# Where the accumulating transfers for w_out's sums are issued

## The chip, the cores and the metric

The kernel runs on one NeuronCore of a Trainium2 chip. The metric is the device time of one execution in microseconds (us). The core has five engines that work side by side, each through its own instructions in order: PE (matrix products), DVE and ACT (elementwise work on SBUF, the on-chip memory), POOL (elementwise work, and here also the issue of accumulating DMA transfers) and SP (issue of plain DMA transfers). Sixteen DMA engines carry all transfers. They are fed from two queues that matter here: q1, which SP fills, and q0, which POOL fills. Engines wait for each other through semaphores.

## The reference

One encoder layer on 256 tokens of width 2048, everything in fp32:

```python
hn = rmsnorm(x, norm_w)
q, v, f_fwd, f_bwd, z_a, b_gate, c_gate, h_b, z_b = split(hn @ w_in)   # nine times 2048 columns
o_a = head_rmsnorm(hgrn2_bidirectional(silu(q), v, f_fwd, f_bwd)) * silu(z_a)   # group A
y_b = b_gate * conv3(c_gate * h_b)                                              # group B
o_b = rmsnorm(y_b) * silu(z_b)
h = x + concat(o_a, o_b) @ w_out
h = h + (p @ w_ple) * sigmoid(h @ w_ple_gate)
out = rmsnorm(h, final_norm_w)
```

The weights are 151 MB for w_in, 34 MB for w_out and 17 MB for w_ple_gate; each element is read once and used for 256 tokens.

## The kernel before

**Products.** An fp32 product is made of split operands: a weight tile is cut in a rounded high part and the rest (`split`, line 121 on ACT, line 122 on DVE), the activations likewise, and PE multiplies high by both and rest by high. `Stream` brings the weights: raw tiles of 1 MB in a ring of three (`rawp`, SP's DMAs at lines 96 and 100), split tiles in a ring of five (`splp`). A raw tile can be loaded again only when the last part of the tile three before it has been split, and a split tile only when PE has used what was there. `Stream.get` splits three parts ahead of PE.

**Stages.** First group A (up to about 510 us in the trace), then group B (to about 855 us), then w_out, then the gate. Group B runs over i = 0 to 7, 256 columns each. A *column-major block* is one call of `gemm_in`: 2 MB of weights of one kind (C, h, B or Z) for one i, PE lines 431 and 433, whose loads move 8 KB per partition and packet. Blocks i = 0 and 1 make all four kinds this way. For i = 2, 4 and 6 a *wide block* (`gemm_ch`, `gemm_pair`, `half`, PE lines 560 to 562) makes C and h for i and i + 1 at once: eight raw tiles (quarters), of which the third and the fifth go through a scheme of seven products in place of eight, for which DVE adds weight blocks (line 83) ahead of the last two of their four splits. A wide block's loads move 2 KB packets, those of the two quarters with sums 1 KB packets; a wide block is followed by the column-major blocks B and Z of i and of i + 1. The wide block takes all four of the PSUM banks that the column-major blocks use in turn.

**Sums for w_out.** Four of the eight quarters of each half of w_out also go through seven products. Their weight sums are not made by DVE but by DMA in DRAM, ahead of time: sixteen pairs (`prepared`, tiles `sums{u}_{half}_{q}`). During group A, SP copies the right and left blocks into `sums` (`prepare`, line 337). During group B, POOL issues three accumulating transfers per pair (`add_up`): step 0 adds w_out to two blocks (line 345, 512 KB), steps 1 and 2 add a block of `sums` to another (line 349, 256 KB each). Each step waits on POOL until the pair's step before has landed. In the w_out stage SP loads `sums` as raw tiles.

**Order.** POOL executes in the order in which its instructions stand in the program. `pump()` takes the next of the 48 steps from `steps_up` and places it there; `at(dt, fn)` runs fn after dt ticks, and a tick is one step in PE's list of products (four products in a column-major block, three in most of a wide one). A transfer's place decides behind which POOL instruction it stands; nothing else makes it wait, apart from the landing of the step before. In the kernel before `pump()` stands behind POOL's products of group B (lines 965 to 1002), and four times at ticks 5, 15, 25 and 35 of each wide block (line 948), where POOL has no other work.

Of the kernel before, what the change touches and what calls it, by code (L numbers as in the profile page):

```python
# [137 lines left out]
def tile_hymba_encoder(  # L138
# [75 lines left out]
    oblocks, prepared = [], []  # L214
# [109 lines left out]
    pend = []  # L324
    now, count = [0], [0]

    def at(dt, fn):
        count[0] += 1
        pend.append((now[0] + dt, count[0], fn))
# [9 lines left out]
    def add_up(what, step):  # L339
        (_, right), sums = what  # L340
        if step == 0:
            n = right[0].shape[2]
            for c, src in enumerate(right):
                tc.keep_in_program_order(
                    pool.dma_start(sums[:, 0:3:2, n * c : n * c + n], src, accum_op=ALU.add)
                )
        else:
            dst, src = ((3, 0), (1, 3))[step - 1]
            tc.keep_in_program_order(pool.dma_start(sums[:, dst], sums[:, src], accum_op=ALU.add))


    steps_up = [(4 * g + n, step) for g in range(len(prepared) // 4) for step in range(3) for n in range(4)]

    def pump():
        if steps_up:
            n, step = steps_up.pop(0)
            add_up(prepared[n], step)
# [104 lines left out]
    def gemm_pair(name, sums_of, ids, get):  # L462

        acc = [psg.tile([P, 512], F32, tag="g", name=f"a{name}_{b}") for b in range(4)]
        sc = [t.rearrange("p a b -> p (a b)") for t in scps]

        def extra():
            x, y = (psm.tile([P, 512], F32, tag=t, name=f"e{t}{name}") for t in "xy")
            return [x, y, *sc]

        main = [[acc[m], acc[2 + m]] for m in range(2)]
        for q1, q5, q6, q7 in half(main, extra, VZ_ORDER, sums_of, ids, xs, xq, True):
            vt, zt, d = get()
            with tc.high_priority(offset=400):
                act.copy(out=vt[:, 0], in_=q1)
                dve.tensor_tensor(out=d, in0=vt[:, 0], in1=q6, op=ALU.subtract)
                dve.tensor_tensor(out=zt[:, 0], in0=q5, in1=d, op=ALU.subtract)
                dve.tensor_tensor(out=vt[:, 1], in0=d, in1=q7, op=ALU.subtract)
                dve.tensor_tensor(out=zt[:, 1], in0=zt[:, 0], in1=q7, op=ALU.add)
        with tc.high_priority(offset=400):  # L480
            for n, dst in enumerate((vt, zt)):
                for m in range(2):
                    dve.tensor_tensor(out=dst[:, m], in0=main[m][n], in1=dst[:, m], op=ALU.add)
        return vt, zt
# [9 lines left out]
    def evac(acc, dst, tmpp, offset=200):  # L494

        with tc.high_priority(offset=offset):
            for m in range(2):
                r = tmpp.tile([P, T], F32, tag="r", name="r", bufs=2)
                act.copy(out=r, in_=acc[m][:, 1, :])  # L499
                dve.tensor_tensor(out=dst(m), in0=acc[m][:, 0, :], in1=r, op=ALU.add)  # L500
# [10 lines left out]
    with tc.manual_schedule(engines={ENG.Activation, ENG.DVE, ENG.PE}):  # L511
        for g in range(4):
            for c in range(3):
                half, v = ws.open(ids3[c][g])

                n = 2 if g or c else 1
# [309 lines left out]
    last_two, kept = [None], []  # L826
# [104 lines left out]
    def convolved(i, ut):  # L931

        for ii in (i, i + 1):
            tp = psm.tile([P, 2, T], F32, tag="xy"[ii % 2], name=f"ut{ii}")
            for h in range(2):
                c = (2 * (ii % 2) + h) * P
                for m in range(2):
                    pe.transpose(tp[:, h, m * P : (m + 1) * P], ut[:, m, c : c + P], ident)
            act.copy(out=ub[ii % 2][:, :, 1 : T + 1], in_=tp)

    def gemm_ch(i):

        def get():
            a, b = (bp.tile([P, 2, 512], F32, tag=f"late{e}", name=f"ch{i}_{e}") for e in range(2))
            return a, b, early[:, 0:512]

        for z in range(4):
            at(5 + 10 * z, pump)
        a, b = gemm_pair(f"ch{i}", CH_SUMS, blocks[B_CG, i], get)
        with tc.high_priority(offset=300):  # L950
            for m in range(2):
                dve.scalar_tensor_tensor(
                    out=a[:, m], in0=a[:, m], scalar=rx2[:, m : m + 1], in1=b[:, m], op0=ALU.mult, op1=ALU.mult
                )
        at(12, lambda: convolved(i, a))

    for i in range(8):
        u = ub[i % 2]
        if i < 2:
            cg = ctmp.tile([P, 2, T], F32, tag="cg", name=f"cg{i}", bufs=2)  # L960
            evac(gemm_in(B_CG, i, {} if i else TURNED), lambda m: cg[:, m, :], ctmp)
            hb = ctmp.tile([P, 2, T], F32, tag="hb", name=f"hb{i}", bufs=2)
            evac(gemm_in(B_HB, i, {} if i else TURNED), lambda m: hb[:, m, :], ctmp)
            by_norms(cg, rbc2, 2)
            pump()
            pool.tensor_tensor(out=u[:, :, 1 : T + 1], in0=cg, in1=hb, op=ALU.mult)
            pump()
        elif i % 2 == 0:
            gemm_ch(i)
        kick = {} if i % 2 else TURNED  # L970
        hb = ctmp.tile([P, 2, T], F32, tag="hb", name=f"bg{i}", bufs=2)
        evac(gemm_in(B_BG, i, kick), lambda m: hb[:, m, :], ctmp)
        if i >= 2:
            cg = ctmp.tile([P, 2, T], F32, tag="cg", name=f"cg{i}", bufs=2)
        for m in range(2):
            ct = 2 * i + m
            dve.tensor_scalar(cg[:, m, :], u[:, m, 0:T], cvw[:, 0, ct : ct + 1], None, op0=ALU.mult)
            for j in (1, 2):
                dve.scalar_tensor_tensor(
                    out=cg[:, m, :], in0=u[:, m, j : j + T], scalar=cvw[:, j, ct : ct + 1],  # L980
                    in1=cg[:, m, :], op0=ALU.mult, op1=ALU.add,
                )
        pool.tensor_tensor(out=cg, in0=cg, in1=hb, op=ALU.mult)  # L983
        pump()
        y2 = ctmp.tile([P, 2, T], F32, tag="tmp", name=f"y2_{i}")
        act.activation(y2, cg, AF.Square)
        pool.tensor_tensor(out=ysum, in0=ysum, in1=y2, op=ALU.add)
        pump()
        hb = ctmp.tile([P, 2, T], F32, tag="hb", name=f"zb{i}", bufs=2)
        evac(gemm_in(B_ZB, i, kick), lambda m: hb[:, m, :], ctmp, 500 if i in (1, 3, 5) else 200)  # L990
        by_norms(hb, rbc, 2)
        pump()
        sz = ctmp.tile([P, 2, T], F32, tag="tmp", name=f"szb{i}")
        act.activation(sz, hb, AF.Sigmoid)
        for m in range(2):
            ct = 2 * i + m
            dve.scalar_tensor_tensor(
                out=hb[:, m, :], in0=hb[:, m, :], scalar=cnw[:, ct : ct + 1], in1=sz[:, m, :],
                op0=ALU.mult, op1=ALU.mult,
            )  # L1000
        pool.tensor_tensor(out=cg, in0=cg, in1=hb, op=ALU.mult)
        pump()
        if i == 0:
            assert not pend
            actx.close()
            bp = mctx.enter_context(tc.tile_pool(name="bp", bufs=1, side="right", reuse_waits="tile"))
            og = bp.tile([P, 2, 2, 2, P], F32, name="og")
            suma = bp.tile([P, len(SUMS), 3, 2, P], F32R, name="suma")
            mixb.extend(bp.tile([P, 2, 2, T], F32R, name=f"mixb{i}") for i in range(6))
        if i == 6:  # L1010
            mixb.extend(bp.tile([P, 2, 2, T], F32R, tag=f"late{e}", name=f"mixb{i + e}") for e in range(2))
        if i == 2:
            for e in range(2):
                act.copy(out=og[:, e], in_=kept[e])
        hi, lo = mixb[i][:, :, 0, :], mixb[i][:, :, 1, :]
        act.copy(out=hi, in_=cg)
        dve.tensor_tensor(out=lo, in0=cg, in1=hi, op=ALU.subtract)
        for src, z, n in ((mixa, i - 1, len(SUMS)), (mixb, i - SUMS[0], len(sumb32))):
            if 0 <= z < n:
                k = 2 * SUMS[z]  # L1020
                a = ctmp.tile([P, 2, T], F32, tag="tmp", name=f"sa{i}")
                if src is mixb:
                    act_sums(mixb[k // 2], a, sumb32[z])
                else:
                    t = ctmp.tile([P, 4, P], F32, tag="hb", name=f"sb{i}", bufs=2)
                    act_sums(mixa[:, k : k + 2], a, t)
                    act_split(suma[:, z], mixa[:, k : k + 2], t)
# [282 lines left out]
```

## Time and profile before

| | |
|---|---|
| median of 3 runs | 1125.66 us (1125.65 to 1126.28) |
| profiled execution | 1123.09 us, its span 1121.4 us |
| PE busy | 1102.3 us, 98% of the span |
| DVE, ACT, POOL busy | 889.1, 684.9, 246.9 us |
| q1 (SP) | 242.25 MB, 62.1% of the 16 engines' span |
| q0 (POOL) | 16.78 MB, 10.1% |

Views used: the groups of waits, the chain of waits (followed back from the last instruction), the timeline of one engine (start, duration, what it did, and in brackets its idle time ahead and what ended it), the table by stage (length, busy time of each engine, granted TensorE clock, share of DMA engines busy, GB/s) and the DMA view of a stretch (packets, MB and share per queue; then issues by kind with the median time from issue to landing). PE's pieces in the timeline overlap, so its pace is read from the distance of starts.

### The profile page before, as it was taken

The numbers are of one execution on the slowest core, as the hardware profiler recorded it, in microseconds if no ns is written. First come the engines' busy times: TensorE is split into PE (matmuls) and PEld (weight loads), VectorE is DVE, ScalarE is ACT, GpSimd is POOL, SyncE is SP. The second block draws the span as 40 slices with busy tenths as digits, with TensorE's granted clock in tenths as the row PEclk, the third lists the DMA queues.
The fourth block names the chain that finished last, engine by engine and source line by source line (L and its number), as shares of the span: only waits on it lengthen the run. The fifth ranks groups of instructions, "written<-read, shape, count | busy, mean of one in ns | idle before, by whom it ended". The sixth has DMA issues, their size and how long they took to land.

```text
span 1121.4 us, 16647 instructions
## 1 busy us (share of the span) xinstructions
PE 1102.3 (98%) x6269; PEld 939.9 (84%) x6269; DVE 889.1 (79%) x1164; ACT 684.9 (61%) x943; POOL 246.9 (22%) x203
## 2 busy tenths in 40 slices
PE   9999999999999999999998998999999999999996
PEld 8888888888888888888887886887888888888886
DVE  7798588997889788996686797787878879877673
ACT  7696578567866787656444454454556565565562
POOL 1144024203620343053240250132041000000011
PEclk9999999999999999999999998999999999999999
DMA  9886675586548654668887789599779987887532
GB/s 349 322 269 214 219 249 184 176 294 208 187 157 293 227 192 161 215 206 232 232 183 269 212 207 261 193 235 227 257 208 286 339 284 283 301 291 260 201 132 76
DMA packets 83248, 260.43 MB, mean 232 GB/s; under 512 B 8160, under 2 KB 23904, under 8 KB 68704
## 3 DMA queue, kind: packets, MB, share of 16 engines
q1 hardware_dynamic: 73920, 242.25, 62.1%
q0 software_dynamic: 8960, 16.78, 10.1%
q8 instruction: 49, 0.80, 0.3%
q10 hardware_dynamic: 288, 0.34, 0.1%
q14 instruction: 31, 0.25, 0.1%
HBM read 257.25 MB, written 35.65 MB: 261 GB/s over the span
## 4 chain that ended last, share of the span: by engine, by line
PE 90%; DMA 4%; DVE 3%; ACT 2%; SPq 1%; POOL 0%; issue 0%; DVEq 0%; ACTq 0%; POOLq 0%
PE a L433 29%; PE a L431 15%; DMA raw<-in_w_in_dram 3%; PE avz L560 3%; PE avz L562 3%; PE avz L561 3%; PE pg L1071 3%; PE pg L1072 3%; PE pg L1070 3%; PE ach L561 2%; PE ach L562 2%; PE ach L560 2%; DVE spl L122 1%; PE pa L561 1%; PE pa L562 1%; PE pa L560 1%
## 5 line engine op out<-in xcount | busy, mean ns | idle before, releaser
L122 DVE TENSOR_TENSOR spl<-raw,spl 128x1024 fp32r<-128x1024 f32 (+2 forms) x431 | 518.1, 1217 | 148.9 <-ACT spl L121 145.1
L121 ACT CAST spl<-raw 128x1024 fp32r<-128x1024 f32 (+2 forms) x431 | 423.4, 994 | 282.6 <-PE a L431 69.1
L433 PE MATMUL a<-xs,spl 128*128 128x512 f32 x1408 | 483.8, 395 | 0.0
L431 PE MATMUL a<-xs,spl 128*128 128x256 f32 x1408 | 376.6, 278 | 0.0
L433 PEld LDWEIGHTS a<-xs,spl 128*128 128x128 f32 x1408 | 259.9, 188 | 55.3
L431 PEld LDWEIGHTS a<-xs,spl 128*128 128x128 f32 x1408 | 262.5, 188 | 5.6
L560 PE MATMUL ach<-spl,xs 128*128 128x512 f32 x156 | 62.7, 402 | 7.0 <-ACT spl L121 7.0
L1187 POOL TENSOR_TENSOR hh<-hh,fw 128x512 f32<-128x512 f32 (+1 forms) x9 | 11.0, 1228 | 251.0 <-ACT gt L1186 248.4
L561 PE MATMUL ach<-spl,xs 128*128 128x512 f32 x156 | 62.8, 403 | 2.3 <-DVE spl L122 2.3
L562 PE MATMUL ach<-spl,xs 128*128 128x512 f32 x156 | 62.6, 401 | 0.0
L560 PE MATMUL avz<-spl,xs 128*128 128x512 f32 x138 | 54.0, 391 | 0.0
L562 PE MATMUL avz<-spl,xs 128*128 128x512 f32 x138 | 53.7, 389 | 0.0
L561 PE MATMUL avz<-spl,xs 128*128 128x512 f32 x138 | 53.7, 389 | 0.0
L983 POOL TENSOR_TENSOR cg<-cg,bg 128x512 f32<-128x512 f32 x8 | 11.2, 1406 | 189.6 <-DVE bg L500 189.6
L499 ACT COPY r<-a 128x256 f32<-128x256 f32 x88 | 31.5, 368 | 31.8 <-PE a L431 31.7
L1070 PE MATMUL pg<-spl,ht 128*128 128x512 f32 (+1 forms) x120 | 45.2, 377 | 0.0
L1071 PE MATMUL pg<-spl,ht 128*128 128x512 f32 (+1 forms) x120 | 45.0, 375 | 0.0
L1072 PE MATMUL pg<-spl,ht 128*128 128x512 f32 (+1 forms) x120 | 45.0, 375 | 0.0
L733 POOL TENSOR_TENSOR qc<-pf,ge 128x256 f32<-128x256 f32 x16 | 21.0, 1313 | 106.7 <-ACT dd L723 91.8
L560 PEld LDWEIGHTS ach<-spl,xs 128*128 128x128 f32 x156 | 30.4, 195 | 14.7 <-ACT spl L121 8.3
L83 DVE TENSOR_TENSOR raw<-raw 128x512 f32<-128x512 f32 (+1 forms) x45 | 41.2, 915 | 0.8
L122 DVE TENSOR_TENSOR spl<-early,spl 128x1024 fp32r<-128x1024 f32 (+1 forms) x29 | 32.9, 1147 | 9.3 <-ACT spl L121 8.7
(378 smaller groups left out, 1892.5 us busy)
## 6 DMA issues: line engine op xcount, KB each, us to landing
raw<-in_w_in_dram SPq DMA_DIRECT2D x82, 1024.0 KB, 5.0
raw<-in_w_in_dram SPq DMA_DIRECT2D x196, 256.0 KB, 4.4
raw<-in_w_out_dram SPq DMA_DIRECT2D x36, 512.0 KB, 5.7
sums<-in_w_out_dram SPq DMA_DIRECT2D x32, 512.0 KB, 7.1
raw<-in_w_in_dram SPq DMA_DIRECT2D x26, 512.0 KB, 5.8
raw<-sums SPq DMA_DIRECT2D x13, 1024.0 KB, 6.4
raw<-in_w_gate_dram SPq DMA_DIRECT2D x9, 1024.0 KB, 5.6
sums<-in_w_out_dram POOLq DMA_DIRECT2D x16, 512.0 KB, 13.0
```

The lines of the kernel that those rows point to most:

```text
L83: self.nc.vector.tensor_tensor(out=out, in0=out, in1=other, op=ALU.add)
L121: self.nc.scalar.copy(out=v[:, :, 0], in_=r)
L122: self.nc.vector.tensor_tensor(out=v[:, :, 1], in0=r, in1=v[:, :, 0], op=ALU.subtract)
L431: pe.matmul(a[:, :T], lhsT=lhsT, rhs=xs[:, kt, 0, :], start=False, stop=(kt == NKT - 1))
L433: pe.matmul(a, lhsT=lhsT, rhs=xs[:, kt, :, :].rearrange("p s n -> p (s n)"), start=(kt == 0), stop=False)
L499: act.copy(out=r, in_=acc[m][:, 1, :])
L560: pe.matmul(acc, lhsT=ah, rhs=w[:, 0], start=start, stop=False)
L561: pe.matmul(acc, lhsT=ah, rhs=w[:, 1], start=False, stop=False)
L562: pe.matmul(acc, lhsT=al, rhs=w[:, 0], start=False, stop=stop)
L1070: pe.matmul(acc[m], lhsT=lh, rhs=wh, start=(kt == 0), stop=False)
L1071: pe.matmul(acc[m], lhsT=lh, rhs=wl, start=False, stop=False)
L1072: pe.matmul(acc[m], lhsT=ll, rhs=wh, start=False, stop=(kt == nk - 1))
```

## The change

The 48 steps keep their number, kind and size. `steps_up` takes eight pairs in turn, not four, so eight step 0 come ahead of the first step 1. The pumps behind POOL's products and in the wide blocks go away. Instead `pumps(t0, t1, n)` spreads n steps over ticks t0 to t1: 10 and 12 in the four column-major blocks of i = 0 and 1, and 9, 9 and 8 in those that follow the wide blocks of i = 2, 4 and 6.

```diff
-    steps_up = [(4 * g + n, step) for g in range(len(prepared) // 4) for step in range(3) for n in range(4)]
+    steps_up = [(8 * g + n, step) for g in range(len(prepared) // 8) for step in range(3) for n in range(8)]
...
     def gemm_ch(i):
...
-        for z in range(4):
-            at(5 + 10 * z, pump)
         a, b = gemm_pair(f"ch{i}", CH_SUMS, blocks[B_CG, i], get)
...
+    def pumps(t0, t1, n):
+        for z in range(n):
+            at(t0 + (t1 - t0) * z // (n - 1), pump)
+
     for i in range(8):
         u = ub[i % 2]
         if i < 2:
+            pumps(2, 55, 10 + 2 * i)
...
             by_norms(cg, rbc2, 2)
-            pump()
             pool.tensor_tensor(out=u[:, :, 1 : T + 1], in0=cg, in1=hb, op=ALU.mult)
-            pump()
         elif i % 2 == 0:
             gemm_ch(i)
+        if i >= 2 and i % 2 == 0:
+            pumps(2, 41, 9 if i < 6 else 8)
...
         pool.tensor_tensor(out=cg, in0=cg, in1=hb, op=ALU.mult)
-        pump()
...
         pool.tensor_tensor(out=ysum, in0=ysum, in1=y2, op=ALU.add)
-        pump()
...
         by_norms(hb, rbc, 2)
-        pump()
...
         pool.tensor_tensor(out=cg, in0=cg, in1=hb, op=ALU.mult)
-        pump()
```

The assertion that nothing is pending at the end of i = 0 gives way to another. The order of instructions on PE, DVE, ACT and SP stays as it is; POOL's alone changes, at three kinds of places.

**Block i = 0.** POOL's work for the last head pair of group A (`kx7`, then `s7`, the masked scores that PE's products `o` read) and for group B's i = 0 (`ub0`). Before:

```order
L739 TENSOR_TENSOR kx7_4678<-kc7_4672,ge7_4659 128x512
L801 TENSOR_TENSOR s7_4891<-early_152 128x256
L966 TENSOR_TENSOR ub0_4621<-cg0_4627,hb0_4763 128x2x256
L345 DMA sums0_0_3_82<-in_w_out_dram 256x1x512
L801 TENSOR_TENSOR s7_4891<-early_152 128x256
L983 TENSOR_TENSOR cg0_4627<-cg0_4627,bg0_4908 128x512
L345 DMA sums0_0_4_83<-in_w_out_dram 256x1x512
```

and with the change:

```order
L739 TENSOR_TENSOR kx7_4679<-kc7_4673,ge7_4660 128x512
L345 DMA sums0_0_3_82<-in_w_out_dram 256x1x512
L345 DMA sums0_0_4_83<-in_w_out_dram 256x1x512
L345 DMA sums0_0_5_84<-in_w_out_dram 256x1x512
L345 DMA sums0_1_2_85<-in_w_out_dram 256x1x512
L345 DMA sums0_1_3_86<-in_w_out_dram 256x1x512
L801 TENSOR_TENSOR s7_4897<-early_152 128x256
L968 TENSOR_TENSOR ub0_4621<-cg0_4627,hb0_4766 128x2x256
L345 DMA sums0_1_4_87<-in_w_out_dram 256x1x512
L801 TENSOR_TENSOR s7_4897<-early_152 128x256
L345 DMA sums0_1_5_88<-in_w_out_dram 256x1x512
L986 TENSOR_TENSOR cg0_4627<-cg0_4627,bg0_4912 128x512
```

With the change five step 0 stand between `kx7` and `s7`, and two more follow ahead of the product with i = 0's B gate (the eighth, pair 1's, stands further up, ahead of group A's last output gate); before, one step 0 stood between the two `s7` and one ahead of `kx7`.

**From i = 0 to i = 1**, POOL with the change (before, one transfer stands between each two of these products):

```order
L1001 TENSOR_TENSOR cg0_4627<-cg0_4627,zb0_5029 128x512
L349 DMA sums0_0_4_83<-sums0_0_4_83 128x512
L349 DMA sums0_0_5_84<-sums0_0_5_84 128x512
L349 DMA sums0_1_2_85<-sums0_1_2_85 128x512
L349 DMA sums0_1_3_86<-sums0_1_3_86 128x512
L349 DMA sums0_1_4_87<-sums0_1_4_87 128x512
L349 DMA sums0_1_5_88<-sums0_1_5_88 128x512
L349 DMA sums0_0_2_81<-sums0_0_2_81 128x512
L504 TENSOR_TENSOR cg1_5150<-cg1_5150,early_152 128x512
L968 TENSOR_TENSOR ub1_4622<-cg1_5150,hb1_5243 128x2x256
L349 DMA sums0_0_3_82<-sums0_0_3_82 128x512
```

Six step 1 and the first step 2 stand ahead of the product by the norms (`cg1`), which `ub1`, the input of the convolution of i = 1, needs.

**From i = 1 to the wide block of i = 2.** Before:

```order
L1001 TENSOR_TENSOR cg1_5146<-cg1_5146,zb1_5429 128x512
L349 DMA sums0_0_5_84<-sums0_0_5_84 128x512
L345 DMA sums0_1_2_85<-in_w_out_dram 256x1x512
L345 DMA sums0_1_3_86<-in_w_out_dram 256x1x512
L345 DMA sums0_1_4_87<-in_w_out_dram 256x1x512
L345 DMA sums0_1_5_88<-in_w_out_dram 256x1x512
L983 TENSOR_TENSOR cg2_5955<-cg2_5955,bg2_5854 128x512
```

and with the change:

```order
L1001 TENSOR_TENSOR cg1_5150<-cg1_5150,zb1_5439 128x512
L349 DMA sums0_1_4_87<-sums0_1_4_87 128x512
L349 DMA sums0_1_5_88<-sums0_1_5_88 128x512
L345 DMA sums1_0_2_89<-in_w_out_dram 256x1x512
L345 DMA sums1_0_3_90<-in_w_out_dram 256x1x512
L986 TENSOR_TENSOR cg2_5965<-cg2_5965,bg2_5860 128x512
```

Between POOL's last product of i = 1 and its first one behind the wide block there stand two small and two large transfers, where one small and four large ones stood. At the wide block of i = 4 it is one large and three small ones, at that of i = 6 three small ones; before, one small and four large ones stood at each.

More of the change, by code (lines that the diff above doesn't have):

```diff
@@ L1001, in tile_hymba_encoder @@
         pool.tensor_tensor(out=cg, in0=cg, in1=hb, op=ALU.mult)
-        pump()
         if i == 0:
-            assert not pend
+            assert kept
             actx.close()
```

## The prediction

> **What bounds the kernel now.** I read the page first, then the groups of waits for PE, then the table by stage over the three wide blocks.
>
> ```profile
> span 1121.4 us, 16647 instructions
> PE 1102.3 (98%) x6269; PEld 939.9 (84%) x6269; DVE 889.1 (79%) x1164; ACT 684.9 (61%) x943; POOL 246.9 (22%) x203
> PE ach L560 <- ACT spl L121: 7.0, 3, 2.7
> PE ach L561 <- DVE spl L122: 2.3, 3, 0.8
> 566.96:614.52 47.56, 44.33 (x188) 36.00 (x187) 36.46 (x44) 22.17 (x27) 8.80 (x8) 0.96 0.88 237
> 659.84:708.93 49.09, 45.65 (x189) 36.91 (x187) 37.89 (x50) 22.61 (x28) 8.80 (x8) 0.93 0.91 240
> 754.26:799.65 45.39, 42.75 (x189) 34.84 (x188) 34.19 (x37) 21.92 (x25) 8.64 (x8) 1.00 0.94 256
> 577.17 0.39 PE L560 MATMUL ach<-spl,xs 128*128 128x512 f32 x1
> 581.25 0.39 PE L560 MATMUL ach<-spl,xs 128*128 128x512 f32 x1
> ```
>
> PE sets the time nearly everywhere. Inside the program it waits 9.3 us, all in the wide blocks, once in each. The three stages do the same work and differ in length, and the third column from the right, the granted clock, says that two of the waits also cost speed afterwards (0.96 and 0.93 against 1.00). A wide block is 62 groups of three products (six quarters of eight, two of seven), 186 starts. The last two rows are 18 starts apart: 4.08 / 18 = 0.2267 us. Unhindered, a block takes 185 x 0.2267 + 0.39 = 42.3 us. So the blocks lose 5.2, 6.8 and 3.1 us, 15.1 in all: the most that this change can give back, as the rest of PE's work is not touched.
>
> The chain of waits says what each block waited for, POOL's timeline what was issued just before:
>
> ```profile
> 582.13 12.10 DMA raw<-in_w_in_dram
> 594.34 1.05 ACT spl L121
> 595.41 1.24 DVE spl L122
> 595.43 0.49 PE L560 MATMUL ach<-spl,xs 128*128 128x512 f32 x1 [2.47 <-ACT spl L121]
> 675.50 11.88 DMA raw<-in_w_in_dram
> 688.57 0.50 PE L560 MATMUL ach<-spl,xs 128*128 128x512 f32 x1 [2.69 <-ACT spl L121]
> 768.23 12.74 DMA raw<-in_w_in_dram
> 574.20 0.82 POOL L349 DMA_DIRECT2D sums<-sums  x1
> 574.75 4.53 POOL L345 DMA_DIRECT2D sums<-in_w_out_dram  x4
> 667.13 0.81 POOL L349 DMA_DIRECT2D sums<-sums  x1
> 667.67 4.53 POOL L345 DMA_DIRECT2D sums<-in_w_out_dram  x4
> 761.98 4.50 POOL L345 DMA_DIRECT2D sums<-in_w_out_dram  x4
> 629.65 1.47 POOL L983 TENSOR_TENSOR cg<-cg,bg 128x512 f32<-128x512 f32 x1 [50.37 <-DVE bg L500]
> ```
>
> In each block the raw tile of the sixth quarter takes 12 us to land, and 6 to 14 us before its issue POOL has issued a burst of 2.36 MB (0.26 + 4 x 0.52). The program places these four at ticks 5 to 35 of the block, but the last row shows that POOL has nothing to wait for there for 50 us, so it issues them at once when the last product of the block before is done. Whatever stands in POOL's queue behind that product goes into the wide block, with the change too.
>
> **The change part by part.** *Bytes and the issue.* Nothing is added or removed: 48 transfers, 16.78 MB. Alone in the queue they cost POOL:
>
> ```profile
> L349 POOL DMA_DIRECT2D sums<-sums x32: 788/816/855, 526.8 to 852.8; - x32
> L345 POOL DMA_DIRECT2D sums<-in_w_out_dram x16: 1037/1852/2859, 492.5 to 763.7; - x16
> 494.41 1.92 POOL L739 TENSOR_TENSOR kx<-kc,ge 128x512 f32<-128x512 f32 x1
> 498.48 1.62 POOL L801 TENSOR_TENSOR s<-early 128x256 f32<-128x256 f32 x1 [2.15 <-DVE early L800]
> 501.90 1.23 POOL L801 TENSOR_TENSOR s<-early 128x256 f32<-128x256 f32 x1
> 508.29 0.38 PE L814 MATMUL o<-vt,s 128*128 128x128 f32 x2
> 529.61 2.29 POOL L1001 TENSOR_TENSOR cg<-cg,zb 128x512 f32<-128x512 f32 x1 [2.04 <-DVE zb L997]
> 547.76 1.30 POOL L966 TENSOR_TENSOR ub<-cg,hb 128x512 f32<-128x512 f32 x1 [9.04 <-DVE hb L500]
> ```
>
> Four large ones in a row took 4.53 us, so 1.13 each. The five ahead of `s` begin when `kx` ends at 494.4 + 1.9 = 496.3 and end at 502.0; with `ub` and the sixth the second `s` ends at 507.1, where it ended at 503.1. PE reads it at 508.29 and a little after: free, with 1.2 us of cover; at the 1.2 us of the lone first issue (the next bound) it is still free, above 1.4 each it would stall PE. I take 0. The seven small ones ahead of `cg1` take 7 x 0.82 = 5.7 us from 531.9 on, where `cg` ends; `ub` had waited 9 us for DVE anyway. Also 0, unless POOL is held there by a landing (the third rival).
>
> *The wide blocks.* Their bursts shrink from 2.36 MB to 1.57 (two of each size), 1.31 and 0.79 MB. Beside a wide block's loads both queues get the same number of packets, and in the column-major blocks, where packets are 8 KB, POOL's queue gets less (stretches 585 to 593, 497 to 500, 517.5 to 535.5, and what the loads want, 544 to 574):
>
> ```profile
> q0 software_dynamic: 543, 1.05, 70.6%
> q1 hardware_dynamic: 548, 1.01, 38.4%
> q1 hardware_dynamic: 85, 0.70, 64.8%
> q0 software_dynamic: 90, 0.18, 40.3%
> q0 software_dynamic: 815, 1.55, 57.4%
> q1 hardware_dynamic: 432, 3.15, 42.8%
> q1 hardware_dynamic: 3961, 5.58, 58.1%
> ```
>
> The first pair is 131 GB/s for POOL's queue and 126 for the loads. Take 1.05 MB out of the second block: 8.0 us less of that. There the last load landed at 675.5 + 11.9 = 687.4; PE, which stood from 688.57 - 2.69 = 685.9 on, needs it by 683.6 to be fed without a gap (1.05 for ACT, 1.24 for DVE as above). With the burst gone 8 us sooner, at about 681, the loads get the last 0.4 MB at full rate: about 683. So 0 lost there, up to 2 if the burst's end moves less. In the third block 1.57 MB less is 12 us sooner; the loads, issued up to 768.2, land by 776 against 779 needed: 0 lost. In the first, 0.79 MB less is 6 us: landing at 591 for 590.5 needed, 0 to 1 lost.
>
> *What comes before the wide blocks.* This is where it may be given back. The loads of a wide block begin 20 us before its products (544.5 for 566.96). With the change POOL's queue has seven large transfers, 3.67 MB, from 498 on; in column-major blocks it moves 1.55 MB in 18 us, 86 GB/s, so they last to 541. Behind them come eight step 1 and six step 2 (3.67 MB more), issued as landings and POOL's place allow, by 563. Before, that stretch (544 to 574) had 1.04 MB of POOL's; now about 3.4 MB meet the loads, which want 5.58 MB in 30 us (186 GB/s) and get 126 for 3.4 / 0.131 = 26 us. The third quarter, 3.1 MB into the row, then lands at 546.5 + 25 = 572 in place of 563. SP's first loads of the block, that tile's splits and the products that need them:
>
> ```profile
> 544.53 8.51 SPq L100 DMA_DIRECT2D raw<-in_w_in_dram  x8
> 567.42 1.05 ACT L121 CAST spl<-raw 128x1024 fp32r<-128x1024 f32 x1
> 579.16 1.22 DVE L122 TENSOR_TENSOR spl<-raw,spl 128x1024 fp32r<-128x1024 f32 x1 [0.26 <-ACT spl L121]
> ```
>
> Its first part was split at 567.42, its fourth by 580.38, with DVE hardly idle in between, and PE used that at 581.25 (above). So 572 is 4.6 us late and PE stands for 4.6 - 0.9 = 3.7 us; what is late after that, the sixth quarter, is hidden by it. Bounds: 0, if POOL's queue drains at its 131 GB/s in the column-major blocks too and is empty by 545; 9 us, if the quarters with sums, whose 1 KB packets are half the size, get half the share. In between I take 3.7. In the first two blocks a broken wait near 3.3 us (2.47 and 2.69 at one product, about 0.8 at the next) cost another 1.9 to 3.4 us of half clock (5.2 - 3.3 and 6.8 - 3.4); with 1.7 for one such stretch the first block loses 5.4, as much as now: gain -0.2 (from -6 to +5.2).
>
> [...]
>
> For the second block the same bill: in the 30 us from 633 POOL's queue has 2.62 MB (five large) where it had 1.57 (six small), all issued by 647, so done by about 658; the third quarter there was split at 660.37 and now lands at 661 to 662: 0 to 3 us late, 0.9 of it covered. I take 1.2 lost of 6.8: gain 5.6 (3.5 to 6.8). Third block: 1.31 MB as before: gain 2.8 (2 to 3.1), 0.3 kept for DVE's wait.
>
> *The end.* The transfers end sooner (831 for 853), and SP's loads of `sums` wait for none of them: 0.
>
> Sum: -0.2 + 5.6 + 2.8 = 8.2 us off the profiled execution's 1123.1 us, which is 1114.9. That execution is 2.6 us under the median of the runs, so **1117.5 us** against 1125.66.
>
> **The rivals.** *All three waits go* and nothing comes instead: 15.1 us, 1110.6. For it: the queue moved 131 GB/s where it could; against it: 86 in the very blocks that now take most of it.
>
> *The wait only moves.* The queue is as deep ahead of the second block as of the first, and both third quarters are late by 5 us: gains -1, 1 and 2.8, about 1123; with the first at its bound 1127. For it: the second block's loads at 637 meet 1.57 MB at once. [...]
>
> *Slower: the first group does not drain.* If POOL's queue gets only 0.18 MB in 3 us, 60 GB/s, through the column-major blocks, the seven large ones last to 559. The eighth pair's step 1 waits on POOL for that landing, with `cg1` and `ub` behind it: `ub` starts 13 us late, DVE stands at the convolution that reads it and its splits with it, of which some 7.5 us are covered. PE loses 5.5, and the first wide block, beside a full queue to its end, some 13 in place of 5.2; less 8.4 from the other two that is 5 us slower, 1130.6. It decides below about 70 GB/s. Against it: the 18 us at 86.
>
> *The change does not do what it says*: the bursts stay in the wide blocks, since POOL runs ahead. They do, at a half to two thirds of the size; were that still too much, about 1122.
>
> **How the numbers follow.** The forecast (one or two of the waits gone, 1113 to 1121) 0.48; all gone 0.20; only moved or too little changed 0.18; slower 0.14. What a measurement can tell from no change is 0.2%, 2.3 us, so faster is below 1123.4: the first two and a little of the third, 0.71; same 0.15; slower 0.14. The range reaches from the floor, 1110.5, to the first block's bound in the third case, 1127.
>
> **What would show it.** Right: granted clock 1.00 in the third wide block and the second, their stages 42.5 to 44 us long, 12-us landings gone; in the first wide block a new wait of `ach` or its sums' banks around 580, behind DVE's split of the third quarter, and POOL's queue busy without a break from 498 to 570. Wrong: PE waits in a column-major block or at `o`; a first wide block of 42.5 us (drained early) or above 52 (not drained); `ub` of i = 1 after 550.

## The result and the profile after

| | before | with the change |
|---|---|---|
| median | 1125.66 us (4 runs, 1125.33 to 1126.28) | 1112.71 us (4 runs, 1112.16 to 1114.36) |
| profiled execution, its span | 1123.09 us, 1121.4 us | 1114.36 us, 1112.6 us |
| PE busy | 1102.3 us | 1099.5 us |

The ratio of the runs is 0.9887 (95% interval 0.9870 to 0.9904): faster by 12.7 us, between 10.8 and 14.6. The forecast was 1117.5 us, its range 1110.5 to 1127. The two profiled executions lie 8.7 us apart, since the one of before was 2.2 us faster than any of its four runs and the one of the change is the slowest of its four. Losses by stage, below, are those of the profiled executions.

The groups of waits for PE in the wide blocks, with the change:

```profile
PE ach L560 <- DVE zb L500: 2.3, 1, 2.3
PE ach L561 <- DVE spl L122: 0.8, 1, 0.8
PE ach L560 <- ACT spl L121: 0.2, 1, 0.2
```

and the three wide blocks in the table by stage (length, then busy time of PE, PEld, DVE, ACT and POOL; then the granted clock, the DMA share, GB/s):

```profile
567.38:611.03 43.65, 42.73 (x188) 34.84 (x187) 36.38 (x44) 22.20 (x27) 6.79 (x6) 1.00 0.86 241
656.35:703.66 47.31, 44.89 (x189) 35.78 (x187) 41.02 (x54) 24.59 (x32) 8.94 (x7) 0.96 0.84 243
748.98:791.18 42.20, 42.20 (x189) 34.93 (x187) 34.37 (x37) 21.98 (x25) 5.36 (x5) 1.00 0.73 221
```

Of the three waits behind a raw tile that takes 12 us, that of the third block is gone, that of the first has shrunk from 3.2 to 1.0 us, and that of the second is gone too, but this block has a wait of a new kind at its start. (It is late from there on, so it needs its sixth quarter later as well; this run alone does not show that its smaller burst would have cost nothing.) An undisturbed block takes 42.17 us (the run without accumulating transfers, below), so the losses of the blocks went from 5.4, 6.9 and 3.2 us to 1.5, 5.1 and 0: 8.9 us less, which is the whole difference of the two executions (8.7) within 0.2 us. Three views show what stands around the second block's start: POOL's timeline (large transfers only), the chain of waits, and PE's timeline.

```profile
575.69 2.74 POOL L345 DMA_DIRECT2D sums<-in_w_out_dram  x2
629.67 3.18 POOL L345 DMA_DIRECT2D sums<-in_w_out_dram  x3
642.10 2.11 POOL L345 DMA_DIRECT2D sums<-in_w_out_dram  x2
```

```profile
630.84 11.88 DMA raw<-in_w_in_dram
642.74 14.85 DMA raw<-in_w_in_dram
657.69 1.06 ACT spl L121
658.77 1.55 DVE spl L122 x2
661.05 0.43 DVE zb L500
```

```profile
661.52 0.50 PE L560 MATMUL ach<-spl,xs 128*128 128x512 f32 x1 [2.28 <-DVE zb L500]
```

The last part of the block's second raw tile lands 14.85 us after its issue (the second of the two transfers shown). DVE, which has to split it, reaches `zb` (the sum that empties the Z block's PSUM banks) only behind those splits, and PE's thirteenth product of the wide block needs such a bank: the last row is PE waiting for it.

### The profile page after: what moved, and what is told of

Read it like the earlier page. It is cut to its first block, busy times and chain, and to the rows that moved or that the text cites. A ratio compares the mean times of both kernels' runs of the same rounds, so it can differ in the third digit from the quotient of the medians.

```text
span 1112.6 us, 16632 instructions
## 1 busy us (share of the span) xinstructions
PE 1099.5 (99%) x6269; PEld 938.1 (84%) x6269; DVE 889.8 (80%) x1164; ACT 684.7 (62%) x943; POOL 248.6 (22%) x203
## 3 DMA queue, kind: packets, MB, share of 16 engines
q0 software_dynamic: 8960, 16.78, 9.3%
## 4 chain that ended last, share of the span: by engine, by line
PE 92%; DMA 4%; DVE 2%; ACT 1%; issue 0%; POOL 0%; SPq 0%; DVEq 0%; ACTq 0%; POOLq 0%
PE a L433 27%; PE a L431 14%; DMA raw<-in_w_in_dram 4%; PE avz L560 3%; PE avz L561 3%; PE avz L562 3%; PE ach L561 3%; PE pg L1070 3%; PE ach L562 3%; PE pg L1071 3%; PE pg L1069 3%; PE ach L560 3%; PE pa L560 2%; PE pa L562 2%; PE pa L561 2%; PE a L452 1%
## 5 line engine op out<-in xcount | busy, mean ns | idle before, releaser
L560 PE MATMUL ach<-spl,xs 128*128 128x512 f32 x156 | 61.6, 395 | 2.4 <-DVE zb L500 2.3
L561 PE MATMUL ach<-spl,xs 128*128 128x512 f32 x156 | 61.7, 396 | 0.9 <-DVE spl L122 0.8
L562 PE MATMUL ach<-spl,xs 128*128 128x512 f32 x156 | 61.5, 394 | 0.0
L121 ACT CAST spl<-early 128x1024 fp32r<-128x1024 f32 (+1 forms) x29 | 28.7, 990 | 19.4 <-PE pb_y L562 7.5
```

The source lines that it names most:

```text
L121: self.nc.scalar.copy(out=v[:, :, 0], in_=r)
L560: pe.matmul(acc, lhsT=ah, rhs=w[:, 0], start=start, stop=False)
L561: pe.matmul(acc, lhsT=ah, rhs=w[:, 1], start=False, stop=False)
L562: pe.matmul(acc, lhsT=al, rhs=w[:, 0], start=False, stop=stop)
```

## The experiments

Each was timed in three rounds beside the kernel before (medians 1125.51 and 1125.22 us in the two sets of runs). "Loss" is the length of a wide block above 42.17 us in the run's own profile.

| run | median us | ratio to before (95%) | loss in block 1, 2, 3 |
|---|---|---|---|
| before | 1125.66 | | 5.4, 6.9, 3.2 |
| the change | 1112.71 | 0.9887 (0.9870 to 0.9904) | 1.5, 5.1, 0.0 |
| order of eight alone | 1113.70 | 0.9885 (0.9868 to 0.9902) | 0.0, 5.4, 0.0 |
| places alone | 1119.94 | 0.9937 (0.9916 to 0.9957) | 5.8, 5.5, 0.0 |
| change and hold | 1112.62 | 0.9876 (0.9861 to 0.9892) | 0.0, 4.3, 0.0 |
| hold, all behind it | 1108.28 | 0.9837 (0.9820 to 0.9854) | 0.0, 1.1, 0.0 |
| order of eight and hold | 1108.58 | 0.9855 (0.9840 to 0.9870) | 0.0, 0.1, 0.0 |
| hold, two large ones later | 1110.38 | 0.9871 (0.9856 to 0.9885) | 0.0, 2.0, 0.0 |
| no accumulating transfers | 1107.87 | 0.9847 (0.9831 to 0.9864) | 0.0, 0.0, 0.0 |
| hold, 7, 7 and 12 | 1107.82 | 0.9847 (0.9832 to 0.9862) | 0.0, 0.0, 0.0 |

The theory after the result: a wide block loses by what POOL's queue holds at two moments, while its first tiles load (before it starts) and while its sixth quarter loads (in it). The rivals were that the order in turns does it all, or the depth of the queue as such, wherever it stands.

**The order of eight alone.** The kernel before, with one line of the change:

```diff
-    steps_up = [(4 * g + n, step) for g in range(len(prepared) // 4) for step in range(3) for n in range(4)]
+    steps_up = [(8 * g + n, step) for g in range(len(prepared) // 8) for step in range(3) for n in range(8)]
```

> Eight pairs in turn, places of the transfers as in the kernel before. At the first wide block there now stand five small transfers (1.31 MB) behind POOL's last product, at the second one small and four large (2.36 MB, as before), at the third five small (1.31 MB). Theory (the size of the burst decides): first and third block lose 0 to 1 us in place of 5.2 and 3.1, the second loses its 6.8 as before; 1117 to 1119 us. Rival (the order does nothing by itself, the places do): about 1125. Rival (it is the whole depth of POOL's queue ahead of a wide block): the first block loses as before, since eight large transfers now stand ahead of it; about 1122.

Measured: 1113.70 us, as fast as the whole change within the intervals. The three blocks, and POOL's bursts at the first and second:

```profile
567.33:609.51 42.18, 42.18 (x189) 34.93 (x188) 36.47 (x44) 22.11 (x27) 7.90 (x8) 1.00 0.86 247
654.83:702.39 47.56, 44.13 (x188) 35.84 (x187) 37.75 (x50) 22.55 (x28) 8.80 (x8) 0.96 0.93 247
747.72:789.91 42.19, 42.19 (x188) 34.92 (x187) 34.42 (x38) 21.94 (x25) 7.74 (x8) 1.00 0.88 258
```

```profile
574.58 4.18 POOL L349 DMA_DIRECT2D sums<-sums  x5
662.66 4.53 POOL L345 DMA_DIRECT2D sums<-in_w_out_dram  x4
```

Five small ones (1.31 MB) cost nothing; the one block that kept the four large ones kept most of its loss, 3.5 us of wait as before, with one stretch at half clock in place of two (5.4 us for 6.9). So the theory holds block by block. Its number was too high: 1117 to 1119 left up to 1 us in the first and third block and the full 6.9 in the second. The rival of the whole depth falls as it was put, since here eight large ones stand ahead of the first block. They are issued one by one from 492 to 549 us, though: what a queue that is deep at the first loads costs is seen in the next run. That one line gives as much as the change does: on top of it, the new places bring nothing that these runs can tell.

**The places alone.** The change with the order of four.

> Four pairs in turn, at the places of the change. Bursts: 1.57 MB (two of each size) at the first wide block as with the change, 1.05 MB (four small) at the second, 0.79 MB at the third; ahead of the second block's loads two large and three small (1.83 MB) where the change has five large (2.62 MB). Theory: the wait that the change has at the start of the second block (2.3 us and a stretch of half clock) goes, the first block still loses about 2 us. But the second step 1 now stands ahead of the first masked scores s7 and waits on POOL for a transfer issued at 496.5 that lands at 504 to 506, the third ahead of the second s7 for one that lands at 508 to 509: PE, which reads s7 at 508.3, waits 1 to 4 us there. In sum 1111 to 1117, with that wait in PE's groups of waits (line 814). Rival (a landing never holds POOL long enough to matter): 1110 to 1111 and no wait at line 814.

Measured: 1119.94 us, above the 1111 to 1117 expected, and still 0.4 to 0.8% faster than before: the places alone take away the third block's loss. The wait at line 814 is there, and POOL held by landings ahead of it; but the second block's wait at its start did not go, and the first block has one too (POOL's timeline, then PE's):

```profile
506.13 0.81 POOL L349 DMA_DIRECT2D sums<-sums  x1 [5.61 <-DMA sums<-in_w_out_dram]
536.31 4.82 POOL L345 DMA_DIRECT2D sums<-in_w_out_dram  x4
635.76 2.12 POOL L345 DMA_DIRECT2D sums<-in_w_out_dram  x2
```

```profile
511.33 0.49 PE L814 MATMUL o<-vt,s 128*128 128x128 f32 x2 [1.54 <-POOL s L801]
574.22 0.50 PE L560 MATMUL ach<-spl,xs 128*128 128x512 f32 x1 [2.10 <-DVE zb L500]
668.11 0.50 PE L560 MATMUL ach<-spl,xs 128*128 128x512 f32 x1 [2.48 <-DVE zb L500]
```

With four in turn the four large ones fall to 536, 10 us ahead of the first block's loads, and two at 636 stand right ahead of the second block's. So 1.83 MB there cost no less than the change's 2.62 (5.5 us for 5.1), and the eight in turn are what keeps a row of large ones away from the first block. Measured here is close to what the prediction had expected of the change itself in its first block: the queue met the first tiles, and PE stood.

The amount alone does not set the loss, though, as the third block of this run says. Four large ones and a small one (2.36 MB) stand ahead of its loads, issued at 729 to 742, as far from its start as the 1.83 MB are from the second block's, and it loses nothing: its second tile lands 4.2 us before the block begins (751.2), that of the second block 1.1 us before (661.4). In the 10 us from the first issue on, all queues together moved 1.73 MB at the second block and 2.11 MB at the third. Why is open.

**The change and a hold.** One more POOL instruction in each wide block, which copies one column of the eighth quarter's raw tile (`hold` is a new tile of one column):

```diff
+        def held():
+            raw = ws.raws[ws.where[blocks[B_CG, i][-1][0]][0]]
+            tc.keep_in_program_order(pool.tensor_copy(out=hold, in_=raw[:, 0:1]))
+
+        at(46, held)
         a, b = gemm_pair(f"ch{i}", CH_SUMS, blocks[B_CG, i], get)
```

> The change, with one more POOL instruction at tick 46 of each wide block: it copies one column of the raw tile of the block's eighth quarter, so POOL's queue is held until that tile has landed, and the burst behind it goes out at 595 to 600 and not at 575. Nothing else moves. Theory: the first block's remaining loss of 2 us goes, the third stays at 0, the second block's wait at its start stays (its five large transfers are issued at 630 to 643 as before): about 1110.7. Rival (what is taken out of the wide block comes back as a wait in the column-major blocks behind it, whose loads begin at 596): 1112.7 or more, with waits of PE at lines 431 and 433.

Measured: 1112.62 us, where 1110.7 was expected. POOL's timeline and the three blocks in the table by stage say why:

```profile
594.93 0.27 POOL L950 COPY hold<-raw 128x1 f32<-128x1 f32 x1 [19.12 <-DMA raw<-in_w_in_dram]
```

```profile
568.51:610.69 42.18, 42.18 (x189) 34.94 (x187) 36.44 (x44) 22.01 (x27) 7.09 (x7) 1.00 0.75 222
656.01:702.51 46.50, 43.46 (x189) 34.54 (x187) 39.28 (x52) 24.05 (x30) 8.98 (x8) 1.00 0.69 218
748.09:790.28 42.19, 42.19 (x188) 34.93 (x187) 34.29 (x37) 21.96 (x25) 5.71 (x6) 1.00 0.68 219
```

The first block's 1.5 us were the burst of 1.57 MB: held until 595, it costs nothing. The second block's burst is held as well and the block still loses 4.3 us, so there the loss is not the burst but the five large ones ahead of its loads. The rival, though the time is near its 1112.7, does not hold: behind the held bursts the column-major blocks take as long as without any (45.3 us from the first wide block to the second, 45.6 for 45.3 to the third). PE has one wait of 1.2 us at line 433, but at 9.2 us, at the program's start. In its sum the run is not to be told from the change: of the 2.3 us that the profiled pair gives in the blocks, the medians show 0.1. The profiled execution of the change holds a stretch at half clock (granted clock 0.996), its other three runs read 0.998, so the profile probably shows a longer loss than the median run has.

**All transfers behind the hold.** As before, with

```diff
-            pumps(2, 41, 9 if i < 6 else 8)
+            pumps(2, 14, (7, 9, 10)[i // 2 - 1])
```

> As the run before, and the transfers of each group all stand right behind that held instruction (7, 9 and 10 of them, 3.15, 3.15 and 2.62 MB, from 597 us on in the first group), so that at 130 GB/s they are through by 621, at 86 GB/s by 634, when the loads of the next wide block begin. Theory: no wait is left in any wide block, granted clock 1.00 in all three: 1107.5 to 1109. Rival (POOL's queue drains slower beside column-major loads, and the second block's first loads meet its rest): as the run before, 1110 to 1111. Rival (seven transfers at once starve the column-major loads): above 1112, waits at lines 431 and 433.

Measured: 1108.28 us, in the theory's range. The second block still loses 1.1 us, in one wait that is new (PE at the first column-major product behind the block, for DVE's sums of C and h):

```profile
698.44 0.47 PE L433 MATMUL a<-xs,spl 128*128 128x512 f32 x1 [0.90 <-DVE ch L483]
```

**The order of eight and a hold.** The kernel before with the order of eight, the hold, and the wide block's four pumps at ticks 47 to 53 in place of 5 to 35.

> The order of eight with the places of the kernel before, and the held instruction at tick 46 with the four transfers of the wide block behind it; one small one stays ahead of it. So the 2.10 MB of large ones leave the second block's first part, and what stands ahead of its loads is six small ones (1.57 MB), as in the run with the order alone. Theory (there the second block's loss of 5.4 us is the burst alone): all three blocks run in 42.2 us, 1108 to 1109. Rival (what stands ahead of the loads counts whatever its size): a wait at the start of the second block or in its third quarter remains, 1111 to 1113.

Measured: 1108.58 us, blocks of 42.18, 42.25 and 42.19 us. In the order of eight at the old places the second block's loss was the burst alone. Six small ones, spread over the 30 us in which its first tiles load, cost nothing.

**Two of the five large ones later.** The change and the hold, and the two large ones at 642 go behind the second block's hold (7 transfers in the group of i = 2 at ticks 2 to 31, two more at tick 2 of the next).

> The run with the change and the held instruction, and of the five large transfers that stand ahead of the second wide block's loads the last two (issued at 642) go behind the next held instruction; three, issued at 630, stay. Theory A (the two at 642 meet the block's first two tiles and make them late): the wait at the block's start and the one in its third quarter go, the block loses 0 to 1 us of the 4.3, 1108.5 to 1110. Theory B (the three at 630 do it, since they are still in the queue when the loads begin at 634): the block loses 3 to 4 us as before, 1112.

Measured: 1110.38 us, block 2 loses 2.0 us: between A and B. The wait at the start is gone, the one in the third quarter stays (the groups of waits):

```profile
PE ach L561 <- DVE spl L122: 1.3, 2, 1.1
```

So the two at 642 are what PE had waited for at the start: without them the second tile lands at 650.2 and not at 656.5. The wait that stays is not for the raw tile of the third quarter: that has landed at 653.0, and DVE first adds its blocks (line 83) at 660.9. What delays DVE is seen beside the run without accumulating transfers (below), whose block starts at nearly the same time (DVE's and POOL's timelines, first this run, then that one):

```profile
657.40 1.21 DVE L122 TENSOR_TENSOR spl<-raw,spl 128x1024 fp32r<-128x1024 f32 x1
657.55 2.21 POOL L504 TENSOR_TENSOR zb<-zb,rbc 128x512 f32<-128x512 f32 x1 [3.17 <-DVE zb L500]
660.45 0.48 DVE L1008 SCALAR_TENSOR_TENSOR zb<-zb,vec,szb 128x256 f32<-128x256 f32 x1 [1.85 <-ACT szb L1005]
660.86 1.22 DVE L83 TENSOR_TENSOR raw<-raw 128x1024 f32<-128x1024 f32 x1
```

```profile
656.42 1.30 POOL L504 TENSOR_TENSOR zb<-zb,rbc 128x512 f32<-128x512 f32 x1 [4.23 <-DVE zb L500]
656.87 1.93 DVE L122 TENSOR_TENSOR spl<-raw,spl 128x1024 fp32r<-128x1024 f32 x1 [0.53 <-ACT spl L121]
658.72 0.47 DVE L997 SCALAR_TENSOR_TENSOR zb<-zb,vec,szb 128x256 f32<-128x256 f32 x1
659.12 1.21 DVE L83 TENSOR_TENSOR raw<-raw 128x1024 f32<-128x1024 f32 x1
```

The three at 630 still make the first two tiles late (landed at 647.5 and 650.2, for 639.5 and 643.7). Their splits stand ahead of the Z block's sums on DVE, which end 1.1 us later; POOL's product of `zb` by the norms then begins behind a split of DVE and takes 2.21 us for 1.30 (where POOL began first, it was the split that took longer, 1.93 for 1.21). DVE stands for `zb`, and the third quarter's additions, which stand behind it, begin 1.7 us late.

**No accumulating transfers.** `pump` takes a step from the list and does nothing with it.

> The change without the 48 accumulating transfers (so w_out is multiplied with sums that lack their second summand): nothing of POOL's queue meets the loads. Theory (all that the transfers cost is lost in the wide blocks): three blocks of 42.2 us and everything else as it was, 1106.5 to 1108. Rival (they also slow the column-major blocks and the end): below 1105.

Measured: 1107.87 us, all blocks 42.17 to 42.19 us. By the medians the kernel before loses 17.4 us to its accumulating transfers (1125.22 us in the same set) and the change, timed in another set, about 4.8, and nearly all of it in the wide blocks: between them the stages of all these runs agree to 0.3 us, and behind the third to 0.4, but for 0.9 us in the w_out stage of the order of eight and hold.

**A better version.** As "all transfers behind the hold", with 7, 7 and 12 in the three groups, and the hold reads the raw tile's last column (`raw[:, 2047:2048]`), which lands last (in the second block of the kernel before, the four parts of that tile landed in the order of their issue, at 691.7, 692.4, 693.1 and 693.7).

> As the run with the early transfers behind the held instruction, with 7, 7 and 12 in the three groups in place of 7, 9 and 10, and the held instruction reads the last column of the raw tile, which lands last. Theory (what was left there, 1.06 us at the end of the second block, came from the ninth and eighth transfers ahead of the column-major loads): that goes, 1107 to 1108.2. Rival (twelve behind the third block are too many): a wait at line 431 or 433 around 790, 1109.

Measured: 1107.82 us, ratio 0.9847 (0.9832 to 0.9862): faster than both kernels, and not to be told from the run without any accumulating transfers. The split in three groups and the column that the hold reads were changed together, so which of the two took away the 1.1 us is not shown. Its blocks:

```profile
568.02:610.20 42.18, 42.18 (x189) 34.92 (x188) 36.37 (x44) 22.00 (x27) 10.21 (x10) 1.00 0.74 219
655.52:697.72 42.20, 42.20 (x189) 34.89 (x188) 37.71 (x50) 22.26 (x28) 9.76 (x10) 1.00 0.67 203
743.04:785.24 42.20, 42.20 (x189) 34.92 (x188) 34.36 (x37) 21.98 (x25) 12.81 (x14) 1.00 0.71 215
```

## Why the prediction was right, and where its steps were not

The time lies in the range, and the forecast of the profiled execution (1114.9 us) is 0.5 us from the profiled 1114.36. That closeness is luck, for two of its three terms were wrong by about 4 us each, with opposite signs (measured: the two profiled executions):

| gain, us | forecast | measured |
|---|---|---|
| first wide block | -0.2 | 3.9 |
| second | 5.6 | 1.8 |
| third | 2.8 | 3.2 |
| sum | 8.2 | 8.9 |

Nor is this pair typical: by the medians the gain is 12.9 us, so the forecast of 1117.5 us was 4.8 us too slow.

*Bytes and the issue*: right. The five large ones ahead of `s` cost PE nothing: no wait at line 814 with the change, where the second `s` ends at 505.5 and not at 507.1. `ub` of i = 1 starts at 548.18, where 547.76 stood before. The places alone show what the step was near: with a landing to wait for at that place, POOL is held 5.6 us and PE 1.5. The end is as predicted too: from the third block's end to the last product it is 312.6 us for 313.0.

*The first block*: the step "what comes before the wide blocks" failed in its size. It let 3.4 MB of POOL's queue meet the first block's loads and the third quarter land at 572. The DMA view of 544 to 574 with the change:

```profile
q1 hardware_dynamic: 4048, 6.29, 61.5%
q0 software_dynamic: 1144, 2.07, 38.5%
```

2.07 MB met them. Ahead of that, the queue drained faster than assumed (from 498 to 536 it moved 4.18 MB, 110 GB/s, where 86 were taken), so the seven large ones had landed at 535.5, not at 541. The quarter in question landed at 565.0, 1.9 us later than before, and the loads behind it had caught up by then, since the ring let them be issued only at 562. What was left in this block is the burst (the run with the hold), for which the prediction gave 0 to 1 us; it measured 1.5.

*The second block*: the same bill gave 1.2 us of loss, and it measured 5.1. The third quarter was not the tile to look at: it landed at 660.4, sooner than the 661 to 662 of the prediction. The second tile was, 657.6 in place of 650.4, since the 1.57 MB at 630 and 1.05 MB at 642 stood right around its issue. Its splits stand ahead of `zb` on DVE, and so the end of the block before was late with it. The prediction had named a wait of this kind, a new one of `ach` with half clock behind it, at 1.7 us for the stretch, but put it into the first block and behind the third quarter's split. With the burst held, taking the large ones away from there in steps (the two, then all) takes the loss from 4.3 to 2.0 and to 1.1 us.

*The third block* and *the wide blocks*' bursts: right. 1.31 MB in a burst of small ones costs nothing, 0.79 MB neither.

*The rivals.* That the wait only moves came true in one block of three. That all go did not, for the change; the better version does that, at 1107.8 us against the 1110.6 worked out, because the kernel before takes 2.6 us more in its median than in its profiled execution. That this too is lost in these blocks is likely, as the granted clock reads 0.991 to 0.992 in most of its runs and 0.993 in the profiled one, but only the latter has a trace. That the first group does not drain was off: the queue moved 110 GB/s, and the rival needed less than 70. That the change does not do what it says was right as a reading: the transfers at the first ticks of the column-major blocks are issued in the wide block, as before; what helps is that they are fewer and smaller there. Either part of the change does that: the order alone leaves bursts of 1.31, 2.36 and 1.31 MB in the three blocks, the places alone 1.57, 1.05 and 0.79. But only with the order of eight does no row of large ones stand right ahead of the first block's loads, and with the places as well, five of them stand ahead of the second's. The engine time of the transfers differed with their places: the packets of the same 16.78 MB took 10.1% of the 16 engines' span before, 9.3% with the change and 8.6% in the run with all transfers behind the hold.

## What to carry to other kernels

Where an engine only issues transfers, their place in the program set no time here (the four at ticks 5 to 35 of the first wide block went out in a row, within 4.53 us from 574.75 on): ask what it has to wait for ahead of them, and if it is nothing, give it something, as the hold does with one column of the tile whose load must go first (POOL stood 19.12 us for it). A transfer that is moved must be followed to the loads that it now stands ahead of, and each of their tiles checked, with the work that stands behind its split on the same engine, not only the tile that was late before. A sum that comes out right can rest on two wrong terms; the table by stage, not the total, says so.

## What the runs showed of the hardware

In the wide blocks of the profiled kernel before, the granted clock reads 0.50 in two stretches, from 597.03 us on for 3.41 and from 689.19 us on for 6.83, and 1.00 in the rest. With the change it reads 0.50 in one, from 662.72 on for 3.41. Each 3.41 us at 0.50 are worth 1.7 us of PE's work (an estimate: half of their length; PE has 10 products in the one from 597.03 on and 17 in 784.77 to 788.18, at 1.00). The table by stage over stretches of that length around a wait (before, the change, the places alone, the change and hold):

```profile
593.62:597.03 3.41, 0.83 (x2) 0.48 (x3) 1.41 (x2) 2.48 (x3) 0.00 (x0) 1.00 1.06 381
597.03:600.45 3.42, 3.42 (x10) 2.67 (x9) 2.19 (x3) 1.99 (x2) 0.00 (x0) 0.50 0.91 307
781.36:784.77 3.41, 1.84 (x7) 1.32 (x8) 2.42 (x2) 2.18 (x3) 0.00 (x0) 1.00 1.06 374
784.77:788.18 3.41, 3.41 (x17) 2.83 (x16) 1.66 (x3) 2.07 (x3) 0.00 (x0) 1.00 0.96 356
```

```profile
659.31:662.72 3.41, 1.20 (x5) 1.02 (x6) 3.41 (x5) 1.86 (x4) 0.84 (x1) 1.00 0.74 243
662.72:666.13 3.41, 3.41 (x10) 2.68 (x9) 1.58 (x3) 1.14 (x2) 1.34 (x1) 0.50 0.83 274
```

```profile
571.71:575.12 3.41, 1.31 (x6) 0.76 (x5) 3.41 (x5) 2.16 (x4) 0.54 (x1) 1.00 1.11 307
663.87:667.28 3.41, 1.76 (x7) 0.86 (x5) 3.41 (x4) 3.41 (x6) 1.43 (x1) 1.00 0.56 181
```

```profile
658.05:661.46 3.41, 1.88 (x8) 1.24 (x7) 3.41 (x5) 2.03 (x4) 0.67 (x1) 1.00 0.81 279
```

Behind the stretches in which PE was busy for 0.83, 1.20 and 1.31 us the clock reads 0.50 in the next one (for 1.31 it is 575.12 to 578.54); behind those with 1.84, 1.76 and 1.88 it stayed at 1.00 (for the last two, 667.28 to 670.70 and 661.46 to 664.88). The length of the wait alone does not say which it is: in the places alone one of 2.10 us was followed by half clock and one of 2.48 was not. Nor did the third block of before, 2.6 us in two waits, lose anything that way, while its first, 3.2 us in two waits, did. Why one wait costs these 1.7 us more and another nothing is not shown by these few rows. When a second stretch at half clock follows the first isn't settled either. In the kernel before, one with 2.78 us of work at half clock was followed by another, in the order of eight alone one with 2.86 was not:

```profile
689.19:692.61 3.42, 2.78 (x7) 2.20 (x8) 2.16 (x3) 2.19 (x3) 0.00 (x0) 0.50 0.95 334
692.61:696.02 3.41, 3.41 (x10) 2.64 (x9) 3.41 (x5) 2.65 (x3) 0.00 (x0) 0.50 0.77 308
```

```profile
684.29:687.70 3.41, 2.86 (x7) 2.31 (x8) 2.00 (x3) 2.03 (x3) 0.00 (x0) 0.50 1.00 335
687.70:691.11 3.41, 3.41 (x17) 2.81 (x16) 3.41 (x5) 2.63 (x3) 0.00 (x0) 1.00 0.73 300
```

A difference of 0.08 us of work is too small to call it the cause; that stays open.
